# Later places in a hand-written agenda: second weight halves of an RWKV-7 recurrence, and the second part of stick-breaking attention

## The chip, the cores and the metric

The kernel runs on one core of one Trainium2 chip. The metric is the device time of one launch in microseconds, lower is better. The core has TensorE (PE, its weight loads PEld), VectorE (DVE), ScalarE (ACT), GpSimd (POOL) and SyncE (SP), which here issues every DMA. Each engine runs its own instructions in program order and waits on semaphores of the others.

## What is computed

One step of a two-layer encoder for 544 tokens (512 of a prompt, 32 of a sample), all in 32-bit floats. Layer 0 is RWKV-7: projections r, k, v, z of width 2048, 32 heads of 64, and a state update per token,

```
S_t = S_{t-1} diag(w_t) - (S_{t-1} kk_t)(kk_t * a_t)^T + v_t k_t^T ;  y_t = S_t r_t
```

then a group norm per head, a SiLU gate and an output projection. From its result one shared key and value set is projected. Layer 1 is stick-breaking attention, 16 heads of 128: z = q k / sqrt(128), log_stay = log_sigmoid(-z) under a strictly causal mask, its reversed cumulative sum along the keys ("tail"), weights = exp(log_sigmoid(z) + tail), weights times values, times a SiLU gate, and an output projection.

## The kernel before, in words

Products with weights are made as three 32-bit products: a weight tile is split into a rounded part `whi` (a cast on ACT, line 231) and the rest `wlo` (a subtraction of two SBUF tiles, line 232, on DVE while layer 0 runs and on POOL in layer 1), and so is the activation. A weight of 1024 rows by 128 columns is loaded in two halves of four blocks of 128 rows (`wfetch`, line 221) and split half by half (`wsplit`). In the recurrence the split halves go around three buffers, each with a hi and a lo tile, so a half takes the buffer of the half three before it. A projection of one weight is 16 quanta of three matmuls (line 560): the eight row blocks for the first 272 tokens, then the eight for the other 272. The first weight half is in use through quantum 11, the second through quantum 15.

The order of nearly all instructions is written by hand: `at(t, fn)` puts a step on an agenda with a due time, `flush` sorts by due time and issues the steps. The due time sets the order on each engine and nothing else. Its unit is a period, one pair of heads in layer 0 (16 pairs) and one head in layer 1 (16 heads). `SHIFT` adds small offsets to some steps of layer 0; projection quanta come 0.0107 earlier by it.

In layer 0 the pairs are pipelined. In period T the PE runs, by due time, the value projection of pair T-1 (T to T+0.5) and the key projection of pair T+1 (T+0.5 to T+1); between their quanta lie the chunk steps of the recurrence of pair T-2 (`plan_c`), eight times `x`, `u`, `s` at every 1/24: `x(n)` multiplies the newest state (line 907), `u(n)` applies the inverse (line 929; ACT copies `vu`, lines 932 and 933), `s(n)` makes the new state (PE line 944, then DVE writes `st`, line 952, which `x(n+1)` needs). `plan_lm` masks products of the keys (DVE, line 689). `plan_b` sends a block of them through DRAM (SP: store line 741, load line 754) to POOL, which inverts 36 blocks of 32x32 in 62 dependent steps (lines 771 and 776, the solve), and the result goes out (line 757) and back into `lm` (line 745). `plan_m` turns that (DVE, line 791, tile `mt`) and multiplies it on the PE (line 797). POOL has one `npt` and one `qp` tile, so a solve begins only when the one before it has ended, has been sent out and its input has been loaded.

`plan_load` (line 536) places the loads and splits of one weight, with t its start:

```
at(t + 0.3 * d * kh, load, kh)
at(t + d + 0.47 * d * kh, split_w, kh)
```

For a key weight of pair p it is called with t = p - 0.95 and for a value weight with t = p + 0.55, both with d = 0.17. The second halves are thus split at p - 0.70 and p + 0.80. Counted inside a period the second key half is split at 0.30 and the second value half at 0.80.

In layer 1 (`plan_att`), for head j: logits on the PE at j + 0.12 and later, softplus in six steps on ACT and DVE for three banks of keys (lines 1605 to 1617: `sph` rounded, `spl` the rest), then `tails` (the cumulative sums as matmuls with triangular and all-ones matrices, line 1633), `add` (DVE, line 1637), `weigh` (exp on ACT, line 1640), `values` (PE, line 1656), `svalues` and the gating (DVE, lines 1667 and 1671). Between them lie the quanta of the key, value and query projections of head j + 1, a third of a period each, so one quantum every 1/48. `tails` needs `spl` of banks 2 and 1 first. The value projection's half is scaled into `vT` on DVE (line 1487) and transposed on the PE at j + 0.697 (line 1409).

Of the kernel before, what the change touches and what calls it, by code (L numbers as in the profile page):

```python
# [21 lines left out]
NE = E // P  # L22
# [65 lines left out]
def tile_encoder(ctx: ExitStack, tc: tile.TileContext, i, o):  # L88
# [130 lines left out]
    def wfetch(n, kh):  # L219
        raw = wp.tile([P, KH, P], F32, tag="wraw", name="wraw", bufs=RBUF)  # L220
        SY.dma_start(raw, wsrc[n][kh * KH * P:(kh + 1) * KH * P].rearrange("(k p) c -> p k c", p=P))
        return raw

    def wsplit(raw):

        n, pool = wcount[0] % (WBUF + WMORE if wmore else WBUF), wp
        wcount[0] += 1
        if n >= WBUF:
            pool = wmore[0]
        hi, lo = (pool.tile([P, KH, P], F32R, tag=f"{nm}{n}", name=nm, bufs=1) for nm in ("whi", "wlo"))  # L230
        A.copy(hi, raw)  # L231
        (V if onV[0] else G).tensor_tensor(out=lo, in0=raw, in1=hi.bitcast(F32), op=ALU.subtract)  # L232
        return hi, lo
# [288 lines left out]
    def at(t, fn, *args):  # L522

        names = fn.__qualname__.split(".<locals>.")[1:]
        name = names[-1]
        alike = name in ("row", "add", "quantum", "x", "u", "s") or (name == "y" and args != (8,))
        key = " ".join([layer[0]] + names + [str(a) for a in args if not alike])
        agenda.append((t + SHIFT.get(key, 0.0), len(agenda), fn, args))
# [4 lines left out]
            fn(*args)  # L533
        agenda.clear()

    def plan_load(idx, t, d=0.17):

        parts = wready[idx] = [None, None]

        def load(kh):  # L540
            parts[kh] = wfetch(idx, kh)

        def split_w(kh):
            parts[kh] = wsplit(parts[kh])
        for kh in range(2):
            at(t + 0.3 * d * kh, load, kh)
            at(t + d + 0.47 * d * kh, split_w, kh)

    def plan_proj(x, idx, t0, t1, evac):

# [563 lines left out]
    n = NE  # L1114
# [54 lines left out]
    at(1.02, open_b)  # L1169
    for p, q in enumerate(pairs):  # L1170
        if p >= 2:
            plan_load(q.kw, p - 0.95)
        if p >= 1:
            plan_load(q.vw, p + 0.55)
        for plan in (plan_a, plan_lm, plan_b, plan_m, plan_v, plan_c, plan_d):
            plan(q)

# [162 lines left out]
    for k in range(NK):  # L1340
# [14 lines left out]
        else:  # L1355
            t = p3.tile([P, T], F32, tag="t3", name="sqt", bufs=4)
# [65 lines left out]
    def plan_zb(j, idx, t0, t1):  # L1422

        st = {}

        def evac(half, ps, s):
            if half == 0:
                st["t"] = p4.tile([P, T], F32, tag="szb", name="szb", bufs=2)
            u = p4.tile([P, HT], F32, tag="nsq", name="sgm", bufs=2)
            A.activation(u, ps, AF.Sigmoid)  # L1430
            V.tensor_tensor(st["t"][:, s], ps, u, ALU.mult)
        plan_load(idx, t0 - 0.2, 0.1)
        plan_proj(xb, idx, t0, t1, evac)

        def store():
            SY.dma_start(sz_d[j], st["t"])
        at(t1 + 0.05, store)
# [127 lines left out]
    def plan_att(q):  # L1565


        j, t0 = q.j, q.j
# [75 lines left out]
            for step in range(6):  # L1644
                at(t0 + 0.185 + 0.07 * n + 0.03 * step, soft, b, step)
        for n, b in enumerate((2, 1, 0)):
            at(t0 + 0.53 + 0.035 * n, tails, b)
            at(t0 + 0.565 + 0.035 * n, add, b)
            at(t0 + 0.60 + 0.035 * n, weigh, b)
        out = {}  # L1650

        def values(n):
# [7 lines left out]
            TE.matmul(out["s"][:, :DEC], q.cv, z[2][:, 256:288], start=True, stop=False)  # L1660
            TE.matmul(out["s"][:, :DEC], q.v[:, 4], z[2][:, 288:320], start=False, stop=True)
        for n in range(4):
            at(t0 + 0.72 + 0.02 * n, values, n)
        at(t0 + 0.80, svalues)

        def gate():
            V.tensor_tensor(oz[:, j, 0:SEQ], out["p"], q.z[:, 0:SEQ], ALU.mult)  # L1667
        at(t0 + 0.83, gate)

        def sgate():  # L1670
            V.tensor_tensor(oz[:, j, SEQ:T], out["s"][:, :DEC], q.z[:, SEQ:T], ALU.mult)
        at(t0 + 0.85, sgate)

    def plan_xb():
        st = {}
# [25 lines left out]
    n = base  # L1701
    third = 1.0 / 3
# [11 lines left out]
    for j, q in enumerate(heads):  # L1714
        if j == 0:
            plan_k(q, -4.22, -4.005, -0.32)
            plan_v4(q, -4.005, -3.79, -3.74)
            for m in range(NE):
                plan_zb(m, zidx + m, zstart[m], zstart[m + 1])
            at(-0.31, exp_table)  # L1720
        else:
            plan_k(q, j - 1, j - 2 * third, j - 2 * third + 0.03)
            plan_v4(q, j - 2 * third, j - third, j - third + 0.03)
        plan_q(q, j - third, j)
        plan_att(q)
# [6 lines left out]
        A.copy(hi, oz[:, j, :])  # L1732
        (V if j >= 8 else G).tensor_tensor(out=lo, in0=oz[:, j, :], in1=hi.bitcast(F32), op=ALU.subtract)  # L1733
    for j in range(NE):
        at(NE - 1 - third + 0.02 + 0.04 * j if j < 8 else NE - 1 + 0.02 + 0.04 * (j - 8) if j < NE - 1 else NE - 1 + 0.88,
           split_oz, j)
    with tc.manual_schedule():
        flush()
# [57 lines left out]
```

## Time and profile before

| | before |
|---|---|
| median of 3 runs | 1784.86 us (1783.5 to 1788.74) |
| the profiled execution | 1785.67 us, span 1784.0 us |
| mean granted TensorE clock | 0.982 of full speed |
| layer 0's recurrence | about 255 to 875 us, 38 us a period |
| layer 1's heads | from about 1190 us, 31.4 us a head |

A profile here is one execution. For each engine it lists the instructions with their start and duration, and what ended the idle time ahead of them. Of the PE the idle time counts: where it waits for another engine, the time is lost unless other PE work was due.

### The profile page before, as it was taken

What the parts mean: (1) busy time and instruction counts of PE and PEld (TensorE: products, weight loads), DVE (VectorE), ACT (ScalarE), POOL (GpSimd) and SP (SyncE); (2) the same over time, 40 slices, a digit from 0 to 9 for tenths busy, and PEclk for the clock granted to TensorE, in tenths of its full rate; (3) what the DMA queues carried; (4) which work ended last, traced back from release to release, by engine and by line L of the source; (5) the groups of instructions that cost most, each with busy time, mean ns of one, the idle gap of its engine ahead of it and who ended that gap; (6) DMA issues with size and microseconds to landing.
All of it is one profiled execution on the core that took longest, in us unless ns stands there. A gap on an engine that the chain in (4) does not pass through costs nothing. (4 is left out here: it accounts for less than half of the span.)

```text
span 1784.0 us, 38442 instructions
## 1 busy us (share of the span) xinstructions
PE 1675.3 (94%) x15107; PEld 1444.3 (81%) x15107; DVE 765.6 (43%) x1564; ACT 884.9 (50%) x2232; POOL 681.4 (38%) x1371
## 2 busy tenths in 40 slices
PE   5999979999999999999989998999999999999899
PEld 2679867777777777778868998998888888888798
DVE  3674445545555545552355223123443434334400
ACT  2555545565565556555443335254554545555521
POOL 1000276656667666663002443432222222222432
PEclk8999989999999999989999999999999999999999
DMA  8457522333232333332585443433233232323232
GB/s 326 154 160 233 180 76 69 108 84 86 73 80 73 107 80 93 94 89 66 178 287 148 125 142 91 139 106 110 63 85 88 66 107 58 98 75 103 78 111 79
DMA packets 302612, 203.75 MB, mean 114 GB/s; under 512 B 79726, under 2 KB 271872, under 8 KB 300256
## 3 DMA queue, kind: packets, MB, share of 16 engines
q1 hardware_dynamic: 302432, 201.30, 38.2%
q8 instruction: 119, 1.95, 0.5%
q14 instruction: 61, 0.50, 0.1%
HBM read 155.28 MB, written 45.96 MB: 113 GB/s over the span
## 5 line engine op out<-in xcount | busy, mean ns | idle before, releaser
L560 PE MATMUL mm<-x,whi 128*128 128x272 f32 x3584 | 798.4, 315 | 7.0 <-DVE x L1274 3.5
L560 PEld LDWEIGHTS mm<-x,whi 128*128 128x128 f32 x3584 | 572.0, 191 | 70.7 <-issue 23.3
L232 POOL TENSOR_TENSOR wlo<-wraw,whi 128x512 fp32r<-128x512 f32 x198 | 255.2, 1299 | 702.1 <-ACT whi L231 702.1
L560 PE MATMUL mm<-x,wlo 128*128 128x272 f32 x1792 | 520.8, 291 | 1.7 <-POOL wlo L232 1.7
L560 PEld LDWEIGHTS mm<-x,wlo 128*128 128x128 f32 x1792 | 341.3, 190 | 2.4 <-POOL wlo L232 2.4
L231 ACT CAST whi<-wraw 128x512 fp32r<-128x512 f32 x324 | 195.1, 618 | 138.1 <-issue 78.4
L771 POOL TENSOR_TENSOR qtmp<-npt,qp 108x84 f32<-108x84 f32 (+23 forms) x496 | 194.0, 391 | 77.9 <-DMA npt<-nd_d 38.4
L776 POOL TENSOR_TENSOR qp<-qp,qtmp 108x84 f32<-108x84 f32 (+23 forms) x496 | 194.7, 393 | 37.9
L232 DVE TENSOR_TENSOR wlo<-wraw,whi 128x512 fp32r<-128x512 f32 x126 | 88.9, 707 | 116.3 <-ACT whi L231 114.6
L260 PE MATMUL mm<-x,whi 128*128 128x272 f32 x512 | 101.2, 293 | 2.8 <-POOL x L1733 1.4
L932 ACT COPY vu<-ch 64x64 f32<-64x64 f32 (+1 forms) x128 | 27.5, 215 | 133.7 <-PE ch L929 133.4
L952 DVE SCALAR_TENSOR_TENSOR st<-ch,gc,sgc 128x64 f32<-128x64 f32 x128 | 35.7, 279 | 128.2 <-PE ch L944 125.0
L260 PEld LDWEIGHTS mm<-x,whi 128*128 128x128 f32 x512 | 81.7, 190 | 3.9 <-POOL x L1733 1.8
L560 PE MATMUL mm<-xrh,whi 128*128 128x272 f32 x240 | 73.0, 304 | 1.6 <-ACT rout L1087 1.4
L260 PE MATMUL mm<-x,wlo 128*128 128x272 f32 x256 | 74.5, 291 | 0.0
L260 PE MATMUL mm<-yh,whi 128*128 128x272 f32 x256 | 73.9, 288 | 0.0
L260 PE MATMUL mm<-yh,wlo 128*128 128x272 f32 x256 | 73.8, 288 | 0.0
L260 PE MATMUL mm<-yl,whi 128*128 128x272 f32 x256 | 73.8, 288 | 0.0
L560 PE MATMUL mm<-xrh,wlo 128*128 128x272 f32 x240 | 69.3, 289 | 0.3 <-DVE wlo L232 0.3
L560 PE MATMUL mm<-xrl,whi 128*128 128x272 f32 x240 | 69.1, 288 | 0.0
L922 ACT ACTIVATE sgc<-st,gc 128x64 f32<-128x64 f32 x112 | 38.7, 346 | 46.6 <-DVE st L952 46.2
L1640 ACT ACTIVATE z<-z 128x512 f32<-128x512 f32 (+1 forms) x48 | 27.8, 579 | 68.1 <-DVE z L1637 68.1
(322 smaller groups left out, 3180.0 us busy)
## 6 DMA issues: line engine op xcount, KB each, us to landing
wraw<-in_a_w_in_dram SPq DMA_DIRECT2D x128, 256.0 KB
wraw<-in_kv_w_dram SPq DMA_DIRECT2D x68, 256.0 KB
wraw<-in_b_w_in_dram SPq DMA_DIRECT2D x64, 256.0 KB
rca<-rca_d SPq DMA_DIRECT2D x16, 816.0 KB
rca_d<-sgat SPq DMA_DIRECT2D x16, 544.0 KB
x<-in_a_ada_w_dram SPq DMA_DIRECT2D x8, 1024.0 KB
adaw<-in_b_ada_w_dram SPq DMA_DIRECT2D x8, 1024.0 KB
wraw<-in_a_w_out_dram SPq DMA_DIRECT2D x32, 256.0 KB
```

The costliest lines, as they stand in the source:

```text
L231: A.copy(hi, raw)
L232: (V if onV[0] else G).tensor_tensor(out=lo, in0=raw, in1=hi.bitcast(F32), op=ALU.subtract)
L260: TE.matmul(ps[:, :HT], a[:, k % KH, :], b[:, k, s], start=n == 0, stop=n == total - 1)
L560: TE.matmul(ps[half][:, :HT], a[:, k % KH, :], b[:, k, s], start=k + n == 0, stop=k == NK - 1 and n == 2)
L771: G.tensor_tensor(q.tt, q.npt[:, j, j + 1:32].unsqueeze(1).broadcast_to([108, ni, nt]), q.qp[:, 0:ni, j:j + 1].broadcast_to([108, ni, nt]) ...
L776: G.tensor_tensor(q.qp[:, 0:ni, j + 1:32], q.qp[:, 0:ni, j + 1:32], q.tt, ALU.add)
L922: A.activation(sg, state[c], AF.Copy, scale=q.gc[:, c:c + 1])
L932: A.copy(q.vu[64:128, cs, 0, :], pu[64:128, 0:64 * m].rearrange("p (m t) -> p m t", m=m))
L952: V.scalar_tensor_tensor(new, src, gc, ps["g", c], ALU.mult, ALU.add)
L1640: A.activation(z[b][:, :width[b]], z[b][:, :width[b]], AF.Exp)
```

## The change

The second half of a key weight of the recurrence is split at p - 0.57 in place of p - 0.70 (pairs 2 to 15) and that of a value weight at p + 0.895 in place of p + 0.80 (pairs 1 to 15). In attention `tails`, `add`, `values`, `svalues`, `gate`, `sgate` are due 0.03 of a period later, `weigh` 0.025 later, and the split of the last head's `oz` 0.03 later. No instruction is added or taken away, no buffer changes, and all loads keep their places.

```
-    def plan_load(idx, t, d=0.17):
+    def plan_load(idx, t, d=0.17, second=None):
...
-            at(t + d + 0.47 * d * kh, split_w, kh)
+            at(second if kh and second else t + d + 0.47 * d * kh, split_w, kh)
...
-            plan_load(q.kw, p - 0.95)
+            plan_load(q.kw, p - 0.95, second=p - 0.57)
...
-            plan_load(q.vw, p + 0.55)
+            plan_load(q.vw, p + 0.55, second=p + 0.895)
...
-            at(t0 + 0.53 + 0.035 * n, tails, b)
-            at(t0 + 0.565 + 0.035 * n, add, b)
-            at(t0 + 0.60 + 0.035 * n, weigh, b)
+            at(t0 + 0.56 + 0.035 * n, tails, b)
+            at(t0 + 0.595 + 0.035 * n, add, b)
+            at(t0 + 0.625 + 0.035 * n, weigh, b)
...
-            at(t0 + 0.72 + 0.02 * n, values, n)
-        at(t0 + 0.80, svalues)
+            at(t0 + 0.75 + 0.02 * n, values, n)
+        at(t0 + 0.83, svalues)
...
-        at(t0 + 0.83, gate)
+        at(t0 + 0.86, gate)
...
-        at(t0 + 0.85, sgate)
+        at(t0 + 0.88, sgate)
...
-        at(NE - 1 - third + 0.02 + 0.04 * j if j < 8 else NE - 1 + 0.02 + 0.04 * (j - 8) if j < NE - 1 else NE - 1 + 0.88,
+        at(NE - 1 - third + 0.02 + 0.04 * j if j < 8 else NE - 1 + 0.02 + 0.04 * (j - 8) if j < NE - 1 else NE - 1 + 0.91,
            split_oz, j)
```

## Rows read from the trace of the kernel before

**Rows 1.** Waits of the PE, whole span: who waited, total us, times, longest us

```profile
PE ch L907 <- DVE st L952: 21.9, 17, 1.8
PE at L1633 <- DVE spl L1617: 9.1, 15, 0.6
...
PE aux L797 <- DVE mt L791: 7.9, 15, 5.3
```

**Rows 2.** Timeline, one recurrence period: start us, duration us, instruction, idle before and releaser

```profile
499.33 0.62 ACT L231 CAST whi<-wraw 128x512 fp32r<-128x512 f32 x1 [0.51 <-PE mm L560]
...
499.98 0.69 DVE L232 TENSOR_TENSOR wlo<-wraw,whi 128x512 fp32r<-128x512 f32 x1 [1.15 <-ACT whi L231]
...
501.39 0.27 DVE L952 SCALAR_TENSOR_TENSOR st<-ch,gc,sgc 128x64 f32<-128x64 f32 x1
...
501.72 0.33 PE L907 MATMUL ch<-st,ar 64*64 64x64 f32 x4 [1.35 <-DVE st L952]
```

**Rows 3.** Timeline of the PE: the first and the last of thirteen such waits

```profile
270.47 0.33 PE L907 MATMUL ch<-st,ar 64*64 64x64 f32 x4 [1.41 <-DVE st L952]
...
733.00 0.33 PE L907 MATMUL ch<-st,ar 64*64 64x64 f32 x4 [1.50 <-DVE st L952]
```

**Rows 4.** Timeline around the second value half, same period

```profile
519.33 0.69 DVE L232 TENSOR_TENSOR wlo<-wraw,whi 128x512 fp32r<-128x512 f32 x1 [3.10 <-ACT whi L231]
...
521.61 0.75 PE L797 MATMUL aux<-mt,lm 32*32 32x32 f32 x34 [0.19 <-DVE mt L791]
```

**Rows 5.** Timeline where the two halves are split after the change, same period

```profile
504.24 0.21 ACT L933 COPY vu<-ch 64x64 f32<-64x64 f32 x1
...
505.51 0.28 DVE L952 SCALAR_TENSOR_TENSOR st<-ch,gc,sgc 128x64 f32<-128x64 f32 x1 [1.05 <-PE ch L944]
...
506.10 0.33 PE L907 MATMUL ch<-st,ar 64*64 64x64 f32 x4
...
524.02 0.28 DVE L952 SCALAR_TENSOR_TENSOR st<-ch,gc,sgc 128x64 f32<-128x64 f32 x1 [2.01 <-PE ch L944]
```

**Rows 6.** Stretches of the PE: bounds, us, busy us (instructions), granted clock, DMA share, GB/s

```profile
421.70:425.00 3.30, 1.79 (x23) 1.00 0.00 0
425.20:428.50 3.30, 3.30 (x33) 0.50 0.64 165
```

**Rows 7.** Timeline of the PE: the same matmul in three periods, one after the other

```profile
406.14 0.75 PE L797 MATMUL aux<-mt,lm 32*32 32x32 f32 x34 [0.19 <-DVE mt L791]
...
445.72 0.75 PE L797 MATMUL aux<-mt,lm 32*32 32x32 f32 x34 [0.19 <-DVE mt L791]
...
483.67 0.75 PE L797 MATMUL aux<-mt,lm 32*32 32x32 f32 x34 [0.19 <-DVE mt L791]
```

**Rows 8.** Timeline of POOL and of the DMA queue: one solve and the start of the next

```profile
481.10 0.24 POOL L771 TENSOR_TENSOR qtmp<-npt,qp 108x31 f32<-108x31 f32 x1 [2.61 <-DMA npt<-nd_d]
...
510.22 0.23 POOL L776 TENSOR_TENSOR qp<-qp,qtmp 108x11 f32<-108x11 f32 x1
...
511.81 2.52 SPq L757 DMA_DIRECT2D qd_d<-qp  x3
...
519.63 0.49 POOL L771 TENSOR_TENSOR qtmp<-npt,qp 108x31 f32<-108x31 f32 x1 [2.92 <-DMA npt<-nd_d]
```

**Rows 9.** Timeline of one attention head: tails, the last add, the value transposes

```profile
1328.73 0.41 PE L560 MATMUL mm<-x,whi 128*128 128x272 f32 x2
...
1329.11 0.37 PE L1633 MATMUL at<-sph,ntri 128*128 128x256 f32 x1
...
1330.08 0.39 PE L1633 MATMUL at<-spl,ntri 128*128 128x256 f32 x1 [0.60 <-DVE spl L1617]
...
1334.78 0.69 DVE L1637 TENSOR_TENSOR z<-at,z 128x512 f32<-128x512 f32 x1 [0.94 <-PE at L1633]
...
1335.96 0.44 DVE L1487 TENSOR_TENSOR vT<-mm,rstd 128x272 f32<-128x272 f32 x1 [0.49 <-PE mm L560]
...
1336.52 0.60 PE L1409 MATMUL aux<-ident,vT 128*128 128x128 f32 x4
```

## The prediction

> **What bounds the kernel.** I read the list of the PE's waits first, since the PE is busy nearly all the time and only its idle time can be won without removing work. Three entries of it lie where the change works: the recurrence's `x` step waits 21.9 us for the new state `st`, attention's `tails` wait 9.1 us for `spl`, and line 797 waits for `mt` [rows 1]. Then I read one recurrence period in order of time to see what makes `st` late. ACT sits 0.51 us before a cast until a projection matmul releases the buffer; the subtraction behind it holds DVE idle for 1.15 us and runs 0.69 us; `st` is queued behind on DVE and starts at 501.39; the PE has waited 1.35 us when it starts at 501.72 [rows 2]. The cast is the second key half, due at 0.30 of the period, while the buffer's old content (the first value half) is read through quantum 11, due at 11/32 less 0.011 = 0.33. The engines queue behind a buffer, not behind work.
>
> **Part 1, second key half, from 0.30 to 0.43.** Of the 17 waits for `st`, thirteen stand at this place, in periods 2 to 14, the first 1.41 and the last 1.50 us, each 1.33 to 1.53 [rows 3]; they sum to 18.7 us. The other four, 3.2 us in all, follow no second half of the recurrence and stay. Without the subtraction DVE is free from 498.83 (its idle time begins there, 499.98 - 1.15 [rows 2]), does the one queued step ahead of `st` (about 0.9 us) and writes `st` by about 500.0, before the PE gets to 501.72 - 1.35 = 500.37. At the new place the buffer has been free for some 5 us (0.33 against 0.43 of 38 us, less the queue), so no wait for it moves along. What is queued behind now: on ACT nothing urgent follows the two `vu` copies; the cast would run from about 504.4 to 505.0 and the subtraction to 505.7, into DVE idle time of 1.05 us before the next `st`; that `st` slips from 505.51 to about 505.6 and ends at 505.9, and its reader starts at 506.10 [rows 5]. I take no new wait. Gain 18.7 us, with ends 0 (the wait only changes its step) and 18.7.
>
> **Part 1, second value half, from 0.80 to 0.895.** Here the subtraction starts after 3.10 us of idle DVE and pushes `st` and the two `mt` transposes; the PE loses 0.19 us at line 797, in 14 periods [rows 4]: 2.6 us (the longest wait, 5.3 us [rows 1], is pair 0's and is not reached). At the new place DVE is idle 2.01 us before the next `st` [rows 5], longer than the subtraction's 0.69. Gain 2.6, ends 0 and 2.6. The loads keep their order on SP, and the raw tiles are free long before their next load, so no queue is passed.
>
> **The clock.** Right after one of the thirteen waits (PE busy 1.79 of 3.30 us) the granted clock is 0.50, that is 1.2 GHz, with the PE busy throughout; four of the thirteen are followed so, of which one is shown [rows 6]. The period with such a fall takes 445.72 - 406.14 = 39.58 us, against 521.61 - 483.67 = 37.94 without [rows 4, 7]; less the 0.16 by which its wait was longer, a fall costs 1.5 us. No stretch as idle remains in these periods, so I take all four away: 6.0 us, ends 0 and 6.0.
>
> **What is late next: the solve.** Freed, the PE would want a period of 37.94 - 1.35 - 0.19 = 36.4 us. POOL's solve is a chain with a period of its own: first step 481.10, last 510.22 + 0.23 = 510.45, which is 29.35 us; SP sends the result from 511.81, and 7.82 us later, at 519.63, the next solve starts [rows 8]. If SP sent at once, the chain would need 37.2 us here; over the other solves (13 handed on like this one) the same two pieces come to 36.9 on average. So POOL falls 0.5 us behind in each period: 6.0 us over the twelve from 3 to 14. Against this stands the slack it has now: 511.81 - 510.45 = 1.36 us in which its result waits for SP, and some of the time by which the block is back before `mt` reads it, which I put at 0.6 (an estimate, no row shows its landing). Cost 6.0 - 2.0 = 4.0 us, seen as line 797 waiting for `mt` and that for a DMA. Ends: 0, and 9.4 if a moved subtraction stops the solve for its own 0.69 us (worked out with the rivals).
>
> A collision bears on this. The solve's first step took 0.49 us when it started beside the subtraction that ends at 520.02 [rows 4], and the same step 0.24 at 481.10 [rows 8]; so a subtraction slows POOL by 0.25 us at least. The key half's lies within the solve before and after; the value half's moves from the solve's first steps to 2.5 us within it, which I count as no change. The Trainium skill (SBUF — State Buffer, "Who interferes with whom") says that a VectorE instruction with two SBUF inputs shuts out a GpSimd instruction that reads SBUF for its whole length, whichever comes second waiting. By that rule, which the step of 0.49 us bears out in kind, the value half's subtraction may now stop the solve for its full 0.69 us.
>
> **Part 2, attention.** Ahead of `tails` a quantum takes 1329.11 - 1328.73 = 0.38 us; the first `spl` matmul then waits 0.60 [rows 9], in 15 heads, 9.1 us in all [rows 1]. Quanta are 1/48 = 0.0208 apart and one stands at 1/3 + 10/48 = 0.5417; the next is at 0.5625. Moving `tails` from 0.53 to 0.56 passes exactly one. `spl` hangs on ACT's and DVE's own chain and does not move, so the wait shrinks by 0.38 and 0.22 stays: 15 x 0.38 = 5.7 us, ends 0 and 9.1. The order on ACT and DVE does not change. The place to watch is the last third: the last `tails` now passes two quanta, so only one quantum instead of three lies between it and the end of the value projection, and `vT` queues behind the last `add`. The tails end five quanta ahead of the transposes now, at 1336.52 - 1.90 = 1334.62; the add starts 0.16 later, and it and `vT` take 0.69 and 0.44 [rows 9], so `vT` ends about 1.29 after the tails at the latest. The transposes that need its second half are the third and fourth, three quanta and about 0.2 us behind, 1.34: next to nothing is left. I take no wait. `values`, `svalues` and the gates shift by one quantum against the rest; the next user of their accumulators, due at 0.873, stays behind the gate at 0.86. The last head has no next head's quanta to pass, its order stays: nothing.
>
> **Sum.** 18.7 + 2.6 + 6.0 - 4.0 + 5.7 = 29.0 us off the profiled execution's 1785.67 (span 1784.0): 1756.7. That execution is 0.8 above the median of the runs, 1784.86, so against the median I say **1756 us**.
>
> **The rivals.**
> - The solve chain keeps up (more slack than 2.0 us, or faster steps with DVE less crowded). For it: POOL is idle 2.6 and 2.9 us ahead of its solves. Against: that idle time is the hand-over itself, it ends with a DMA [rows 8]. Then 33 us go: 1752; with all 9.1 of attention 1749.
> - The solve chain binds harder. If the value half's subtraction stops it for its own 0.69 us [rows 4] in place of 0.25, its period is 36.9 + 0.44 = 37.35 us, 0.95 behind: 12 x 0.95 - 2.0 = 9.4 in place of 4.0, so 1762; if the falls of the clock stay in part too, 1766. For it: the 0.49 us step. Against: POOL is often between short steps.
> - The wait changes its step: the subtraction at 0.43 holds the next `st` by more than the 0.3 us between its end and its reader [rows 5], about as it does now. Price: 18.7 and 6.0 come back, the solve costs nothing, 8.3 are left: 1777. Against: DVE is idle there for longer than the subtraction.
> - Slower than before. The solve becomes the bound outright: its period would have to pass the mean period before, 38.4 us with the falls in, by what the rest gains (5.7 in attention, 2.9 in period 2: 8.6 over twelve periods, 0.7), so from 39.1 us, a solve longer by 2.2 us. At 2.8 longer, 39.7 us, it is 12 x 0.6 = 7 us slower: 1792. For it: DVE and POOL do slow each other. Against: it needs some six collisions of 0.4 us more per solve, where the change moves two subtractions.
>
> That the edit does nothing is excluded: its buffer is free at both new places.
>
> **How the numbers follow.** Forecast 0.50, chain keeps up 0.15, chain binds harder 0.22, wait changes its step 0.08, slower 0.05. The range from 1749 to 1768 takes in the first three with the ends of attention. A measurement here tells about 0.3%, 5.4 us. All of the first three are faster, and the fourth if part 2 works: faster 0.90, same 0.06, slower 0.04.
>
> **What would show it.** At x(3) of periods 2 to 14 the PE no longer waits for `st`; the cast no longer waits for the PE; the clock stays 1.00 from period 3 to 14; `tails` wait about 0.22 us; line 797 waits for `mt`, by a few tenths, from about period 5, while SP sends the solve's result as soon as it ends. Wrong it would be if `st` is late at `x(4)`, if line 797 waits over 1 us each period, or if the transposes of `vT` wait.

## The result, and the profile after

The changed kernel takes **1763.6 us**, the median of 3 runs (1763.34 to 1769.07), against 1784.86: a ratio of 0.9872, 95% interval 0.9832 to 0.9912. The prediction was 1756 us, from 1749 to 1768: faster, as said, and within the range, but 21.3 us are gained where the sum made 29. Nearest to it is the rival in which the solve chain binds harder, 1762 us. Three runs leave the gain between 15.7 and 30.0 us, so the miss of 7.6 us is itself not clear of the noise; what came otherwise than forecast is read from the traces. The profiled execution took 1763.34 us, its span is 1761.6 us.

First the PE's waits over the whole span, total us, times, longest us, to be read beside [rows 1].

```profile
PE aux L797 <- DVE mt L791: 14.3, 20, 7.2
...
PE at L1633 <- DVE spl L1617: 5.0, 15, 0.6
...
PE ch L907 <- DVE st L952: 4.4, 4, 1.8
```

The wait for `st` falls from 17 times to 4: the thirteen of [rows 3] are gone, and the four that are left lie outside their periods, one at 265.8 us and three between 753 and 765. The tails wait 5.0 us instead of 9.1. In their place line 797 waits 14.3 us instead of 7.9. 7.2 of it is pair 0's, as 5.3 was before; that one lies between 4.6 and 7.9 in all kernels below but the one with the longer hand-over, whichever part is undone.

Next the timeline of one period: what stands at `x(3)` now, where the PE waited 1.35 us, and the key half at its new place.

```profile
453.04 0.28 DVE L952 SCALAR_TENSOR_TENSOR st<-ch,gc,sgc 128x64 f32<-128x64 f32 x1 [0.16 <-PE ch L944]
...
453.54 0.33 PE L907 MATMUL ch<-st,ar 64*64 64x64 f32 x4
...
456.17 0.62 ACT L231 CAST whi<-wraw 128x512 fp32r<-128x512 f32 x1
...
456.82 0.77 DVE L232 TENSOR_TENSOR wlo<-wraw,whi 128x512 fp32r<-128x512 f32 x1 [0.54 <-ACT whi L231]
...
457.51 0.27 DVE L952 SCALAR_TENSOR_TENSOR st<-ch,gc,sgc 128x64 f32<-128x64 f32 x1
...
457.93 0.33 PE L907 MATMUL ch<-st,ar 64*64 64x64 f32 x4
```

Neither matmul group has a bracket, that is, idle time ahead of it. The cast has none either, so the buffer was free. DVE's idle time before the next `st` takes the subtraction in, nearly to the edge: `st` follows with no idle time and its reader starts at 457.93 unhindered.

The same view around the solve, with the DMA queue's own lines (SPq):

```profile
427.66 0.23 POOL L776 TENSOR_TENSOR qp<-qp,qtmp 108x11 f32<-108x11 f32 x1
...
427.91 2.51 SPq L757 DMA_DIRECT2D qd_d<-qp  x3
...
435.37 0.24 POOL L771 TENSOR_TENSOR qtmp<-npt,qp 108x31 f32<-108x31 f32 x1 [2.56 <-DMA npt<-nd_d]
...
435.88 0.97 DVE L791 STREAM_TRANSPOSE mt<-lm 32x288 f32<-32x288 f32 x2 [1.40 <-DMA lm<-qd_d]
...
436.33 0.24 POOL L776 TENSOR_TENSOR qp<-qp,qtmp 108x30 f32<-108x30 f32 x1
...
436.50 0.21 PE L797 MATMUL aux<-mt,lm 32*32 32x32 f32 x2 [0.78 <-DVE mt L791]
...
436.96 1.04 POOL L776 TENSOR_TENSOR qp<-qp,qtmp 108x29 f32<-108x29 f32 x1
...
437.24 0.66 DVE L232 TENSOR_TENSOR wlo<-wraw,whi 128x512 fp32r<-128x512 f32 x1
```

The solve ends at 427.66 + 0.23 = 427.89 and SP sends at 427.91: it waits for the solve now, where in [rows 8] the solve's result waited 1.36 us for SP. The PE waits 0.78 for `mt`, which waited for the block's return (`lm<-qd_d`). In pairs 2 to 13 DVE sits idle for that DMA ahead of the transposes ten times, 10.7 us in all. The last two lines are the value half at its new place: POOL's step, 0.24 us a moment earlier on about the same size, takes 1.04 beside a subtraction of 0.66. It starts 0.28 us ahead of the subtraction and ends 0.10 us behind it.

And stretches of the PE: bounds, us, busy us (instructions), granted clock, DMA share, GB/s.

```profile
470.90:474.20 3.30, 2.17 (x18) 1.00 0.45 105
474.40:477.70 3.30, 3.30 (x50) 0.50 0.00 0
...
586.90:590.20 3.30, 1.88 (x48) 1.00 0.07 20
590.40:593.70 3.30, 3.30 (x55) 0.50 0.02 5
...
290.00:740.00 450.00, 439.64 (x5546) 0.97 0.34 87
```

In the stretch ahead of 474.2 line 797 waited 0.96 us, in the one ahead of 590.2 1.35 us, and right after each the granted clock is 0.50, 1.2 GHz, with the PE busy throughout. A third fall, at 665.4, comes after a wait of 0.59 us there, while none follows the 0.78 us at 436.50. Between 290 and 740 us, 23.9 us run at this level; before it was 10.2. The falls did not go, they now come behind line 797 and no longer behind `x(3)`.

Where the 22.4 us of the span went: the recurrence, from the first to the last matmul of line 907, is 597.8 us (256.2 to 854.0) against 614.7, 16.9 less. From head 0's tails to head 15's it is 467.6 against 474.0, 6.4 less. What is left nearly cancels: +0.4 ahead of the recurrence, +1.8 between the two and -1.2 at the end.

### The profile page after: what moved, and what is told of

It reads as the page before. It is cut to its first block, busy times and chain, and to the rows that moved or that the text cites. A ratio compares the mean times of both kernels' runs of the same rounds, so it can differ in the third digit from the quotient of the medians.

```text
span 1761.6 us, 38443 instructions
## 1 busy us (share of the span) xinstructions
PE 1670.9 (95%) x15107; PEld 1442.0 (82%) x15107; DVE 764.1 (43%) x1564; ACT 881.3 (50%) x2232; POOL 680.5 (39%) x1371
## 4 chain that ended last, share of the span: by engine, by line
PE 69%; ACT 8%; DVE 8%; DMA 5%; issue 4%; POOL 3%; SPq 2%; POOLq 0%; ACTq 0%; DVEq 0%
PE mm L560 32%; PE mm L260 10%; PE at L1633 3%; PE at L1583 3%; PE aux L1656 2%; DMA lm<-qd_d 2%; PE aux L685 2%; POOL qtmp L771 2%; PE pada L186 2%; POOL qp L776 2%; DMA qd_d<-qp 2%; ACT junk L1454 2%; PE ch L929 2%; PE ch L944 1%; PE ch L907 1%
## 5 line engine op out<-in xcount | busy, mean ns | idle before, releaser
L560 PEld LDWEIGHTS mm<-x,whi 128*128 128x128 f32 x3584 | 570.3, 190 | 70.5 <-issue 23.9
```

What stands on the lines that cost most here:

```text
L560: TE.matmul(ps[half][:, :HT], a[:, k % KH, :], b[:, k, s], start=k + n == 0, stop=k == NK - 1 and n == 2)
```

## The experiments

A "period" is the distance of two pairs' line 797, for pairs 2 to 13. Diffs are against the changed kernel unless the text says otherwise; gains are against the kernel before on the same chip, and where two kernels ran on different chips their gains are compared and not their times (the changed kernel gains 21.3 us).

### Attention alone

```
-            plan_load(q.kw, p - 0.95, second=p - 0.57)
+            plan_load(q.kw, p - 0.95)
...
-            plan_load(q.vw, p + 0.55, second=p + 0.895)
+            plan_load(q.vw, p + 0.55)
```

> Attention's steps late, both weight halves of the recurrence at their old places. Theory (each part acts for itself, tails pass one quantum): the head period falls from 31.40 to about 31.0 us, the tails' wait from 0.60 to 0.32 a head, the recurrence is as before; 6 to 7 us off, about 1778. Rival (attention's gain needs the earlier recurrence, or is a clock effect): under 2 us off.

Measured: 1779.97 us, ratio 0.9972 (0.9963 to 0.9982), 5.4 us less than the 1785.36 of the kernel before. The tails wait 5.0 us, as in the changed kernel. Part 2 is worth about what its term says.

### The recurrence's two halves alone

Attention's times are those of before:

```
-            at(t0 + 0.56 + 0.035 * n, tails, b)
+            at(t0 + 0.53 + 0.035 * n, tails, b)
...
```

> Both second halves late, attention as before. Theory: x(3) no longer waits, line 797 waits some 7 us in place of 2.6 because the solve chain is late, SP sends each result within 0.1 us of the solve's end; about 15 us off, 1770. Rival (only the clock keeps the gain below the forecast, the chain is not late): line 797 waits under 3 us in all.

Measured: 1765.86 us, ratio 0.9905 (0.9881 to 0.993), 19.5 us less. This and attention's 5.4 come to 24.9, against the whole change's 21.3: the parts add up within what a measurement tells. Line 797 waits 12.8 us, and 20.5 us between 290 and 740 run at 1.2 GHz. The disturbance at line 797 belongs to the recurrence's edits.

### The key half alone

As the last, and the value half back at p + 0.80:

```
-            plan_load(q.vw, p + 0.55, second=p + 0.895)
+            plan_load(q.vw, p + 0.55)
```

> Only the second key half late. Theory: nearly all of e2's gain, since line 797 waits for the solve chain anyway and what the value half delays is hidden behind that: within 3 us of e2. Rival (the parts simply add): the 0.19 us of the value half at line 797 stays in 14 periods, on top of a chain that is not late, and e3 is 2.6 us or more slower than e2 with no DMA in front of the mt transposes.

Measured: **1759.74 us**, ratio 0.987 (0.9847 to 0.9892). Against both expectations it is faster by 6.1 us than with the value half moved too (four runs each; the two intervals just touch). The waits:

```profile
PE aux L797 <- DVE mt L791: 7.9, 15, 5.2
...
PE ch L907 <- DVE st L952: 4.6, 6, 1.8
```

Line 797 is back at what it was before the change: pair 0's 5.2 and 0.19 in each of the others. The twelve periods are all 36.5 or 36.6 us; in the changed kernel they go from 35.9 to 40.1. And the stretch between 290 and 740:

```profile
290.00:740.00 450.00, 441.49 (x5685) 1.00 0.35 92
```

No fall of the clock is left in it. The timeline where the value half is split shows why the solve fares better:

```profile
397.91 0.69 DVE L232 TENSOR_TENSOR wlo<-wraw,whi 128x512 fp32r<-128x512 f32 x1 [3.10 <-ACT whi L231]
397.99 0.71 POOL L771 TENSOR_TENSOR qtmp<-npt,qp 108x31 f32<-108x31 f32 x1 [2.61 <-DMA npt<-nd_d]
```

The subtraction meets the solve's first step and costs it 0.71 - 0.24 = 0.47 us; at the new place it cost 1.04 - 0.24 = 0.80 in the row above. Over pairs 2 to 13 the solve, from its first step's start to its last one's end, takes 28.9 us here and 29.3 with the value half moved too. With a hand-over of 7.6 us from SP's issue to the next start the chain needs 36.5 against 36.9, and the PE wants about the same 36.5 (the forecast's working had 36.4). The 0.4 us decide which of the two leads: in the changed kernel the `mt` transposes wait for their DMA in ten of twelve pairs, here in none. It is a near tie all the same, since here too SP sends each result within 0.12 us of the solve's end.

### The value half alone

Attention and the key half as before, so that the diff against the kernel before is this alone:

```
-            plan_load(q.vw, p + 0.55)
+            plan_load(q.vw, p + 0.55, second=p + 0.895)
```

> Only the second value half late. Theory: the key half still stalls x(3), so the period stays near 38 us, the chain has its slack, line 797's 0.19 us goes: 2 to 3 us off, about 1782, with x(3) waiting some 19 us as before. Rival (the value half carries the gain): 8 us or more off.

Measured: 1773.57 us, ratio 0.9942 (0.9923 to 0.9961): 11.8 us less, four times what was expected. Ten of twelve periods are 37.3 to 37.5 us, against 37.9 to 38.2 without a fall in the kernel before: 0.5 us a period and not 0.19. The timeline of the kernel before around its value half, now with the weight loads (PEld) that were left out in [rows 4]:

```profile
520.27 0.20 PEld L907 LDWEIGHTS ch<-st,ar 64*64 64x64 f32 x4 [0.31 <-DVE st L952]
...
521.17 0.14 PEld L797 LDWEIGHTS aux<-mt,lm 32*32 32x32 f32 x2 [0.23 <-issue]
...
521.61 0.64 PEld L797 LDWEIGHTS aux<-mt,lm 32*32 32x32 f32 x34 [0.30 <-DVE mt L791]
```

and the same place in the kernel with the value half moved:

```profile
516.61 0.97 DVE L791 STREAM_TRANSPOSE mt<-lm 32x288 f32<-32x288 f32 x2
...
516.91 0.20 PEld L907 LDWEIGHTS ch<-st,ar 64*64 64x64 f32 x4 [0.15 <-issue]
...
517.74 0.65 PEld L797 LDWEIGHTS aux<-mt,lm 32*32 32x32 f32 x36
517.75 0.76 PE L797 MATMUL aux<-mt,lm 32*32 32x32 f32 x36
```

The 36 loads now run in one go. In the kernel before, the subtraction made `st` late by 0.31 us for the loads of line 907, and the loads of line 797 sit idle for 0.23 us (the row names no releaser) and 0.30 us behind `mt`, while the PE's own lines show 0.19 only; the ends of its matmuls are modelled. 0.31 + 0.23 + 0.30 = 0.84 us less the 0.15 left is an upper end, the period gained 0.5. That these waits make up the 0.5 is argued from the rows and not shown by a run of its own. Over the twelve periods that makes 452.2 us against 461.1, 8.9 less, of which some is the clock's, with 6.8 us at 1.2 GHz between 290 and 740 instead of 10.2; the periods ahead of and behind the twelve (40.0 against 41.3, 41.1 against 43.1) bring the rest of the 11.8. As long as the key half stays where it was, the period is 37.5 us, above the chain, and nothing is lost to the longer solve: all this is gained.

### Key half and attention, the value half undone

```
-            plan_load(q.vw, p + 0.55, second=p + 0.895)
+            plan_load(q.vw, p + 0.55)
```

> The changed kernel with the value half put back to its old place (key half and attention stay late). Theory: the value half's subtraction, moved into the solve, costs the solve 0.35 us a period and makes its chain (36.8) longer than the PE's period (36.5); without it the chain keeps up, line 797 waits 0.19 only, the granted clock stays at 1.00 from period 3 to 14, and the time is e3's less attention's 6: about 1753 us, 10 faster than the changed kernel. Rival (e3 was quick by a luck of the clock): 1760 to 1764 with falls of the clock in the recurrence.

Measured: 1756.42 us, ratio 0.984 (0.9802 to 0.9878), a gain of 29.6 us, 8.3 more than the changed kernel's. Periods 36.5 to 36.7, the solve 28.6 on average, no low clock between 290 and 740:

```profile
290.00:740.00 450.00, 441.51 (x5686) 1.00 0.35 92
```

The recurrence takes 589.6 us (256.7 to 846.3) against 597.8. Twice now, with attention's edits and without, undoing the value half has won 6 to 8 us.

### A solve made longer, in the kernels before and after

Three of the 31 products of the solve are made twice, which changes no value and adds about 1.2 us to it:

```
+            if j in (9, 12, 15):
+                G.tensor_tensor(q.tt, ...)
```

In the kernel after:

> The changed kernel with three steps of each solve done twice (same result), about 1.2 us more on POOL per solve. Theory: the chain is the bound, so the period grows by about as much, to 38.0, and line 797's waits by about 12 us: 1773 to 1780 us. Rival (POOL has room): under 3 us more.

In the kernel before:

> The kernel before with the same three steps done twice. Theory: there the PE's own stall sets a period of 38.0 to 38.4 us and SP picks up the result 1 to 2 us after the solve ends, so 1.2 us more are mostly covered: 0 to 4 us slower. Rival (a longer solve costs the same in both): 12 us or more slower.

Measured: after 1781.2 us, ratio 0.9977 (0.9956 to 0.9997), a gain of 4.8 us where the changed kernel has 21.3, so 16.5 lost; before 1785.67, ratio 1.0003 (0.9983 to 1.0022). The same 1.2 us a solve cost nothing in the kernel before and about 16.5 us in the one after, somewhat above the 12 x 1.2 = 14.4 of the chain, with 44.4 us at 1.2 GHz between 290 and 740. Line 797 (now 800, behind three added lines) in the kernel after:

```profile
PE aux L800 <- DVE mt L794: 18.4, 15, 7.9
```

So the chain has no slack left after the change. Before it had about as much as the longer solve takes: SP, which sent the results 0.75 to 2.98 us after their end in pairs 2 to 13, now sends seven of the twelve 0.03 us after it.

### A shorter hand-over, which became a longer one

In the kernel after, the three DMAs that bring the solve's input and the three that take its result become one each:

```
-            SY.dma_start(q.npt[36 * g:36 * g + 36], nd)
+            if g == 0:
+                SY.dma_start(q.npt.rearrange("p s t -> p (s t)"),
+                             nd.rearrange("m s t -> m (s t)").unsqueeze(0).broadcast_to([3, 36, 1024]))
...
-            SY.dma_start(qd.rearrange("m (i g) t -> g m i t", g=3)[g], q.qp[36 * g:36 * g + 36])
+            if g == 0:
+                SY.dma_start(qd.rearrange("m (i g) t -> g m i t", g=3), q.qp)
```

> The changed kernel, all of it, with the solve's hand-over shortened: the three stores of its result as one DMA and the three loads of its input as one DMA. Theory (the chain of solve, store, load is the bound): from the store's issue to the next solve 7.6 us falls to about 6, line 797's waits outside pair 0 fall from 7 to under 1 us, the period goes to about 36.0, falls of the clock mostly go, the time is 1745 to 1752. Rival (the chain is not what line 797 waits for, or single DMAs land later): no gain, 1762 or more.

Measured: 1883.48 us, ratio 1.0549 (1.05 to 1.0599). It was expected to gain. The timeline of POOL and the DMA queue:

```profile
513.65 0.74 SPq L760 DMA_DIRECT2D qd_d<-qp  x1
514.90 3.78 SPq L755 DMA_DIRECT2D npt<-nd_d  x1
520.58 3.02 SPq L745 DMA_DIRECT2D lm<-qd_d  x4
...
527.84 0.24 POOL L774 TENSOR_TENSOR qtmp<-npt,qp 108x31 f32<-108x31 f32 x1 [6.68 <-DMA npt<-nd_d]
```

The store is issued in 0.74 us instead of 2.51, but its block can be fetched only 520.58 - 513.65 = 6.93 us later, in most periods 6.4, against 432.26 - 427.91 = 4.35 in the changed kernel. The load, whose own issue takes 3.78 us instead of 1.27 for the three, takes 12.94 us from issue to the solve's start, mostly 11.8 to 12.3, against 435.37 - 430.61 = 4.76. So the hand-over is 14.2 us here, mostly 13.1, and not 7.6, with a solve still of 29.3. The stretches while the load moves say why; bounds, us, PE's busy us, granted clock, DMA share, GB/s, first with the one load:

```profile
520.00:523.00 3.00, 3.00 (x26) 1.00 0.29 82
```

and in the changed kernel with three:

```profile
432.00:433.00 1.00, 1.00 (x10) 1.00 0.65 238
```

The DMA engines are busy for 0.29 of their time instead of 0.65, at a third of the rate; other DMAs share both stretches. Counted by size, the load is 108 packets of 4096 bytes. The one load's start three at a time and take 7.05 us, from 519.48, when the store's last ones go, to 526.53; they keep 0.19 of the DMA engines busy. In the changed kernel the three loads' take 2.65 us, from 431.64 to 434.28, at 0.54.

The Trainium skill (DMA: Bandwidth & Descriptors, "Why a DMA increments its semaphore by 16 and not by 1") has a DMA spread over the largest number of engines, 16 at most, that divides the slowest dimension of both its sides: by it 12 for each old load, with 36 on both, and 3 for the new one, with 108 and 3, an estimate of 0.75 and 0.19 of the engines. The 0.19 agrees; the 0.54 is a mean in which the three loads begin and end, and comes to 0.64 at its busiest.

The periods are 44.3 to 46.1 us, line 797 (800 here) waits 81.4 us in all, and the clock falls in every period. The experiment did not shorten the chain as it was meant to. That a longer chain makes the kernel slower agrees with the chain's lead.

### Tails one quantum later still

```
-            at(t0 + 0.56 + 0.035 * n, tails, b)
-            at(t0 + 0.595 + 0.035 * n, add, b)
-            at(t0 + 0.625 + 0.035 * n, weigh, b)
+            at(t0 + 0.575 + 0.035 * n, tails, b)
+            at(t0 + 0.61 + 0.035 * n, add, b)
+            at(t0 + 0.64 + 0.035 * n, weigh, b)
```

> The changed kernel with tails, add and weigh another 0.015 of a head period later, so that the first tails pass one more quantum. Theory (each quantum passed takes what is left of the wait for spl, which hangs on ACT and DVE alone): the wait of 0.32 a head goes to 0, the head period from 31.01 to about 30.7 us, 4.8 us off the changed kernel: about 1759. Rival (another wait takes its place: the transposes of vT, or values for weigh): under 1.5 us off, with a new PE wait at line 1409 or 1656 in every head.

Measured: 1756.54 us, ratio 0.9844 (0.9828 to 0.9861), a gain of 26.3 us, 5.0 more than the changed kernel's and as much as its tails still waited. The wait for `spl` has left the list of waits, and one head takes 30.6 us, against 31.0 after and 31.4 before.

### The best of both

The two last edits that gained, together:

```
-            plan_load(q.vw, p + 0.55, second=p + 0.895)
+            plan_load(q.vw, p + 0.55)
...
-            at(t0 + 0.56 + 0.035 * n, tails, b)
+            at(t0 + 0.575 + 0.035 * n, tails, b)
...
```

> The value half back at its old place (as in e5) and the tails another quantum later (as in e9). Theory (the two act in different phases and add): e5's time less 4.8 us, 1750 to 1752, faster than the kernel before and the changed one. Rival (they do not add): within 2 us of e5.

Measured: **1748.46 us** (1746.06 to 1750.88), ratio **0.9804** (0.9788 to 0.982): a gain of 34.4 us, 13 more than the change's. Against the last kernel, which ran on the same chip and differs by the value half alone, it is 8.1 us faster, and here the intervals are clear of each other: the third time that undoing the value half wins. Its waits, and the stretch between 290 and 740:

```profile
PE aux L797 <- DVE mt L791: 7.8, 15, 5.1
...
PE ch L907 <- DVE st L952: 4.2, 4, 1.8
```

```profile
290.00:740.00 450.00, 441.48 (x5685) 1.00 0.35 92
```

Both gains stand together: periods of 36.5 to 36.7 us, heads of 30.6. Second buffers for the solve's input and result, meant to take the hand-over off the chain, were not tried.

## Why the prediction was right or wrong

**Second key half: right.** All thirteen waits went, none came at `x(4)`, and the edge there is as narrow as the prediction's shifted times made it: the subtraction ends at 457.59, `st` starts at once. With it alone the twelve periods sum to about 439 us instead of 461, 22 less. The forecast's share for them is 12 x 1.44 = 17.3 of waits and three falls of 1.5: 21.8.

**Attention: right.** 5.7 us were forecast, 5.4 measured by itself, 6.4 between the first and the last tails. The timeline of one head after, to be read beside [rows 9]:

```profile
1313.39 0.39 PE L1633 MATMUL at<-spl,ntri 128*128 128x256 f32 x1 [0.32 <-DVE spl L1617]
...
1319.10 0.43 DVE L1487 TENSOR_TENSOR vT<-mm,rstd 128x272 f32<-128x272 f32 x1
1319.47 0.60 PE L1409 MATMUL aux<-ident,vT 128*128 128x128 f32 x4
```

The tails wait 0.32 us and not 0.22, and the transposes of `vT` have no idle time ahead of them. The waits alone give 15 x 0.28 = 4.1 us; a head takes 0.39 us less, and where the other 0.11 us of each lies is not shown. That the next quantum would have taken the rest too was not seen: moving by one more won 5 us.

**What is late next: right in kind.** SP sends the solve's result 0.03 us after its end in nine of the twelve periods, and line 797 waits for `mt` and `mt` for a DMA, as written. The pair of longer solves shows that the chain has no slack after and had some before.

**Second value half: failed as a part**, twice over. "Gain 2.6" was read from the PE's own rows at line 797; the weight loads showed more, and by itself the edit gains 11.8 us. And its subtraction "moves from the solve's first steps to 2.5 us within it, which I count as no change". Over pairs 2 to 13 the POOL steps beside it now take 0.69 us more, on average, than the shortest of the same steps; with the value half undone it is 0.38 without attention's edits and 0.15 with them, where the subtraction mostly runs ahead of the first step, in the hand-over. The solve takes 29.1 to 29.3 us with the value half moved and 28.6 to 28.9 with it undone, which is what puts the chain, at 36.8, above the 36.5 that the PE wants. So beside the key half its sign turns, and undoing it gains 6 to 8 us. The rival "the solve chain binds harder" named this place; it priced the chain at 37.35 us, half a microsecond above what came, and had the falls of the clock only as a remark (1766).

Against the kernel before, though, the solve did not grow: 29.1 us in both. Moving the key half alone shortens it to 28.9, which the prediction did not reckon with, and the value half gives that back. So the chain of 36.9 us came out nearly right, in part by luck: that average takes in pair 14's 39.9 us, and over pairs 2 to 13 the kernel before had 36.8.

The trace of before held a better guide to the price than the 0.25 us: the POOL step that starts with the key half's subtraction of [rows 2].

```profile
499.55 0.35 POOL L771 TENSOR_TENSOR qtmp<-npt,qp 108x91 f32<-108x91 f32 x1
...
499.98 0.91 POOL L776 TENSOR_TENSOR qp<-qp,qtmp 108x91 f32<-108x91 f32 x1
```

It takes 0.91 us beside a subtraction of 0.69; undisturbed steps next to it, of like size, take 0.34 to 0.36.

The Trainium skill (SBUF — State Buffer, "Who interferes with whom") has the subtraction shut POOL out for its whole length, here 0.66 to 0.69 us. The step of 1.04 us beside it agrees in that it ends only when the subtraction has; that it had started first does not fit the page's order, by which the second one waits (the profile's spans on POOL are rough). The 0.25 us taken from [rows 4] was small since POOL's first step there had started 0.30 us after the subtraction.

**The clock: the step that failed.** "No stretch as idle remains in these periods, so I take all four away", 6.0 us. It did not reckon with the forecast's own next part: a chain that binds makes new idle stretches, at line 797. Behind three of them, of 0.96, 1.35 and 0.59 us, the clock fell, for 23.9 us in all where it was 10.2 before. Of the 10 us by which the changed kernel's twelve periods exceed those with the value half undone (449 against 439), 7.7 lie in the three periods with falls, 40.1, 38.9 and 39.1 us against 36.8. Each fall lets the solve catch up: right after them, and nowhere else in these periods, SP is late again, by 3.18, 2.07 and 1.63 us. After the first:

```profile
501.49 0.23 POOL L776 TENSOR_TENSOR qp<-qp,qtmp 108x11 f32<-108x11 f32 x1
...
504.90 2.52 SPq L757 DMA_DIRECT2D qd_d<-qp  x3
```

Then the deficit builds up anew, until the next wait and the next fall. That a wait at line 797 brings the fall is read from this order and from the kernels with waits of 0.19 us there, which have no fall between 290 and 740; the two were not taken apart, and the wait of 0.78 us without a fall shows that the wait's length alone does not settle it.

**The sum.** In the recurrence the forecast was 18.7 + 2.6 + 6.0 - 4.0 = 23.3, measured 16.9: most of the 7.6 us by which the time was missed. The term that was missed is the clock's. From the solve of pair 2 to that of pair 14 twelve cycles take 449 us: 442 are solve and hand-over, 6.9 are the three late sends behind the falls. The forecast made 12 x 36.4 + 4.0 = 440.8 of it, so the chain by itself is 1.2 us over and the falls the rest. This is an account from the trace and no experiment. With the value half undone and the tails at 0.56 the gain is 29.6 us against the sum's 29.0, but by other terms: a chain that costs next to nothing and no gain from the value half.

## What to carry to other kernels

When a wait is taken off the leading engine, compare its new period with the cycle of every chain of other engines that feeds it, hand-over included; within half a microsecond of each other, any instruction that slows the chain decides. A VectorE instruction with two SBUF operands is best kept out of a dependent POOL chain, or where the chain has a pause anyway. Measure the parts of a change alone and in pairs: here one part gained 11.8 us by itself and lost 6 to 8 beside the other.

## What the runs showed of the hardware that was not expected

One DMA over 108 partitions in place of three over 36 landed far later: its 108 packets took 7.05 us at 0.19 of the DMA engines instead of 2.65 at 0.54, and from issue to use the load took 12.9 us instead of 4.8. The store's block could be fetched after 6.4 instead of 4.35 us, though its issue took 0.74 us instead of 2.51; the load's issue took 3.78 instead of 1.27. A POOL step beside a VectorE subtraction of two SBUF tiles took 0.91 to 1.04 us instead of 0.24 to 0.36. And idle time of the PE stands partly in the rows of the weight loads alone: 0.31 us at line 907 where the matmul's row shows none.
